# S5 tables built inside the RWKV chain of a hybrid decoder layer, and S5 inputs projected earlier

## The chip, the core and the metric

One NeuronCore of one Trainium2 chip runs the whole layer. The metric is device time in microseconds (us), the median of three runs of the same kernel: 1288.53 us before the change (1288.47 to 1292.1). A prediction is for the same metric of the changed kernel on the same kind of chip.

## What the reference computes

One decoder layer on x of shape (1, 1024, 1024) in float32. A normalised input goes through one combined projection; four head groups of 256 channels use it, their outputs are concatenated and projected, and a squared-ReLU MLP follows:

```python
h = rmsnorm(x, norm_mix_pre[l])
proj = h @ w_in
out_s5 = s5_mixer(s5_u, ...)
out_ret = retention_mixer(ret_q, ret_k, ret_v, ret_g, cos, sin)
out_rw, v_first = rwkv7_mixer(rw_cols, ...)
out_sb = stick_breaking_mixer(sb_q, sb_k, sb_v)
mixed = jnp.concatenate([out_s5, out_ret, out_rw, out_sb], axis=-1) @ w_out[l]
x = x + rmsnorm(mixed, norm_mix_post[l])
h = rmsnorm(x, norm_ffn_pre[l])
f = jnp.square(jax.nn.relu(h @ w_up[l])) @ w_down[l]
x = x + rmsnorm(f, norm_ffn_post[l])
```

The S5 mixer is a complex diagonal recurrence over the sequence, followed by a GELU and a gated linear unit. The kernel does it in blocks of 8 tokens: with powers of the complex diagonal in two tables (RC the real, RS the imaginary part, 128 positions each) the recurrence becomes a real scan between two rotations.

## The kernel before

The program is one long list of instructions that a tile scheduler distributes over the engines. Each engine, and each queue of DMA issues (nearly all are issued by SyncE, "SP"), then works through its own list strictly in order. So an instruction that waits holds back all that stands behind it on its engine.

The order of the stages is this. The input is normalised and transposed (tiles hh and hl, the high and low part of each float32 number). The RWKV columns are projected first. Then comes the RWKV chain: 16 chunks of 64 tokens, one `rwkv_chain` each (lines 587 to 630), a recurrence whose small matmuls (tiles cr, cu, cs, cy) depend on one another over ScalarE, VectorE and GpSimd. During the first half of the chain a second triangular inverse is made (`rwkv_inverse`, lines 507 to 529: VectorE's loop, a store to DRAM, a load back as tile tx, matmuls ix). Then `rwkv_out` (lines 633 to 664) finishes RWKV's two halves of tokens; after that the kernel takes turns between two Python generators, `retention` and `s5_main`, for 14 rounds (lines 2005 to 2015), and goes on with the stick-breaking attention (tiles z, om, be, wt), the output projection and the MLP.

What TensorE does between the links of these chains is filler: the rest of the input projection. It comes from `proj_rest` (six channel groups, then three token groups with index 1, 2, 0, which are retention's v, S5's input u, and the attention's v; then the attention's k and q). Each product is three float32-replicated matmuls (`mm3`, lines 131 to 133). The class `Pace` hands the filler out in small portions (`g.pace.fill(n)`) and counts them in `g.pace.n`: 131 portions when the chain ends, 147 after `rwkv_out`. In the loop of 14 rounds `s5` takes part only once `g.pace.n` has reached 164, that is from the fifth round on.

On-chip memory is handled as slots of [128, 1024] float32, s0 to s40, lent by `M.get(group, ...)` and given back by `M.put`. Twenty of them (s21 to s40) belong to group "R" during RWKV; after `rwkv_out` ten go to "rt" (retention) and ten to "s5". A slot that is lent again makes its new user wait for its last user.

In the first step of `s5_main` the kernel loads u twice (tile un, named s5n; line 1115), copies it (us, line 1117), transposes it with TensorE (s5p, line 1124; uT, line 1125), loads the two tables QT (line 1129) into slots that un has given back, and builds RC and RS on GpSimd: seven doublings, each one complex multiplication (`cmul`, lines 892 to 906), 44 instructions with the two memsets. The second step multiplies QT by uT on TensorE (s5p, line 174 in `Traced`) and VectorE multiplies the result by RC and RS (lines 1164 to 1170).

Of the kernel before, what the change touches and what calls it, by code (L numbers as in the profile page):

```python
# [181 lines left out]
def flat(ap):  # L182
    return ap.rearrange("p a b -> p (a b)")
# [917 lines left out]
def s5_main(tc, g, I):  # L1101
# [10 lines left out]
    us = [M.get(G, [128, 8, 8, 16], F32, "s5u") for _ in range(2)]  # L1112
    for b in range(2):
        un = M.get(G, [128, 8, 8, 16], F32, "s5n")
        SY.dma_start(un.rearrange("p j g c -> p j (g c)"),
                     g.d_u.rearrange("(p j) x -> p j x", j=8)[:, :, 128 * b:128 * b + 128])
        V.tensor_copy(us[b], un.rearrange("p j g c -> p g j c"))
        M.put(un)
    uT = [M.get(G, [128, 8, 128], F32, "s5uT") for _ in range(2)]
    for g0 in range(0, 16, 4):  # L1120
        ps = psw()
        for q in range(4):
            gg = g0 + q
            T.transpose(ps[:, q], us[gg // 8][:, gg % 8].rearrange("p j c -> p (j c)"), g.ident)
        A.activation(uT[g0 // 8][:, g0 % 8:g0 % 8 + 4], ps, AF.Copy)
    M.put(*us)
    QT = [M.get(G, [128, 8, 128], F32, "QT") for _ in range(2)]
    for ri in range(2):
        SY.dma_start(flat(QT[ri]), g.d_qt[ri])

# [12 lines left out]
    M.put(W1, W2)  # L1143
    RH = M.get(G, [128, 8, 128], F32, "RH")
# [660 lines left out]
def kernel(ctx: ExitStack, tc: tile.TileContext, I, out, dbg=None):  # L1805
# [71 lines left out]
    def proj_rest():  # L1877
        for j, col in ((0, 256), (1, 384), (2, 512), (3, 640), (4, 1024), (5, 1152)):
            yield from proj_ch(tc, g, I, col, sink_plain(tc, g, g.d_ret[128 * j:128 * j + 128]))
        yield from proj_tok(tc, g, I, 1, tok, sink_tok(tc, g, g.d_vr))  # L1880
        yield from proj_tok(tc, g, I, 2, tok, sink_tok(tc, g, g.d_u.rearrange("(u p) c -> p u c", p=128)))
# [86 lines left out]
    P.memset(g.ST, 0.0)  # L1968
    ys = []
# [4 lines left out]
    for c in range(NCH):  # L1974
# [11 lines left out]
        if c % 8 == 7:  # L1986
            t = c // 8
            ys.append(g.y)
            M.put(g.AR[0][t], g.AR[1][t], g.BK[0][t], g.BK[1][t], g.UV[2 * t], g.UV[2 * t + 1], g.Aq[t])
    for t in range(2):  # L1990
        rwkv_out(tc, g, t, ys[t])
        g.pace.fill(8)
# [7 lines left out]
    rt, s5 = retention(tc, g, I), s5_main(tc, g, I)  # L2000
    g.we = "AV"
    g.T = Traced(T)
# [8 lines left out]
    for i in range(14):  # L2011
        paced(rt)
        if g.pace.n >= 164:
            paced(s5)
# [184 lines left out]
```

## Time and profile before

| what | value |
|---|---|
| median of the runs | 1288.53 us (1288.47 to 1292.1) |
| the profiled execution | 1289.48 us |
| its span | 1287.3 us |
| mean granted TensorE clock in it | 0.989 |
| TensorE busy | 1233.5 us, 96% of the span |
| VectorE, ScalarE, GpSimd busy | 68%, 47%, 12% |

How to read it: a busy TensorE is one that has a matmul in its pipeline, at whatever clock. The granted clock (PEclk) is a share of the full 2.4 GHz; at 1.2 GHz it reads 0.5. A window of 10 us with 0.83 has thus spent about a third of its time at the lower level. A wait is named by who waited and who released it. Rows of a timeline give start, length, engine, line, operation, tiles and shapes, and in brackets the idle time before it with its releaser; SPq rows are DMA issues, and their length is the time that the issue kept the queue.

### The profile page before, as it was taken

To read this page: it belongs to the slowest core of one execution; us is meant where nothing else is said; L and a number is where in the kernel's file an instruction comes from. 1 tells how busy PE (TensorE), PEld (TensorE's weight loads), DVE (VectorE), ACT (ScalarE), POOL (GpSimd) and SP (SyncE) were. 2 spreads that over 40 slices of the span, in tenths; PEclk is the share of its full clock that TensorE was granted. 3 is DMA by queue.
4 is the path that set the end of the run, shared out by engine and by line. 5 is a ranking of instruction groups with operands and counts; after the bars stand their busy time and mean duration, and the time that the engine had idled before them with its cause. 6 is when DMAs were issued, how large, how long until landed. Compare 5 with 4: busy or idle time off the path is not lost.

```text
span 1287.3 us, 19608 instructions
## 1 busy us (share of the span) xinstructions
PE 1233.5 (96%) x7256; PEld 993.3 (77%) x7256; DVE 870.8 (68%) x1724; ACT 607.8 (47%) x1152; POOL 152.5 (12%) x181
## 2 busy tenths in 40 slices
PE   4999998999989999999999999999999999999997
PEld 4788776778877756778787888888888788888885
DVE  8884676623555236789889768876758576776757
ACT  6453351262412344466666645454555433554541
POOL 1332011102351102433400000000000000000000
PEclk9999998999998999999999999999999999999999
DMA  5121242224655457433541378653379653444433
GB/s 203 66 82 70 74 109 80 76 91 137 197 147 95 148 162 227 126 103 95 163 157 42 99 220 294 212 164 123 138 248 325 219 157 123 115 123 151 146 122 146
DMA packets 129375, 185.93 MB, mean 144 GB/s; under 512 B 37456, under 2 KB 63552, under 8 KB 129280
## 3 DMA queue, kind: packets, MB, share of 16 engines
q1 hardware_dynamic: 129280, 184.68, 45.4%
q8 instruction: 57, 0.93, 0.3%
q14 instruction: 38, 0.31, 0.1%
HBM read 125.94 MB, written 58.70 MB: 143 GB/s over the span
## 4 chain that ended last, share of the span: by engine, by line
PE 71%; DVE 13%; DMA 8%; ACT 4%; issue 2%; POOL 1%; SPq 0%; DVEq 0%; ACTq 0%
PE pu_b L1416 19%; PE pd_b L1701 18%; PE mm_b L131 6%; PE mm_b L132 5%; PE mm_b L133 5%; PE pd_b L1757 3%; DVE om_s L722 2%; DMA wraw_s<-in_w_in_dram 1%; PE mmc_b L131 1%; DMA wraw_s<-in_w_up_dram 1%; PE mmc_b L132 1%; PE mmc_b L133 1%; PE av_b L757 1%; DVE v_s L1385 1%; PE s5p_b L174 1%
## 5 line engine op out<-in xcount | busy, mean ns | idle before, releaser
L1416 PE MATMUL pu_b<-v_s,v_s 128*128 128x512 f32 x1344 | 306.9, 390 | 0.7 <-DVE u_h L1560 0.5
L1416 PEld LDWEIGHTS pu_b<-v_s,v_s 128*128 128x128 f32 x1344 | 251.8, 188 | 54.0 <-DVE u_h L1560 0.9
L1701 PE MATMUL pd_b<-v_s,v_s 128*128 128x512 f32 x1152 | 262.2, 389 | 2.5 <-ACT v_s L1384 2.5
L1701 PEld LDWEIGHTS pd_b<-v_s,v_s 128*128 128x128 f32 x1152 | 216.0, 188 | 48.2 <-ACT v_s L1384 3.3
L131 PE MATMUL mm_b<-hh_s,wh_s 128*128 128x512 f32 (+1 forms) x296 | 122.7, 415 | 1.2 <-DVE xs_s L359 0.5
L132 PE MATMUL mm_b<-hl_s,wh_s 128*128 128x512 f32 (+1 forms) x296 | 117.4, 397 | 0.0
L133 PE MATMUL mm_b<-hh_s,wl_s 128*128 128x512 f32 (+1 forms) x296 | 115.7, 391 | 0.0
L1384 ACT ACTIVATE v_s<-wd_s 128x512 fp32r<-128x512 f32 x112 | 68.2, 623 | 67.9 <-PE pd_b L1701 30.3
L1385 DVE TENSOR_TENSOR v_s<-wd_s,v_s 128x512 fp32r<-128x512 f32 x112 | 75.6, 685 | 22.8 <-ACT v_s L1384 22.2
L1384 ACT ACTIVATE v_s<-fl_h 128x512 fp32r<-128x512 f32 x96 | 59.4, 625 | 66.5 <-PE pd_b L1701 29.4
L1384 ACT ACTIVATE v_s<-wraw_s 128x512 fp32r<-128x512 f32 x96 | 59.0, 628 | 63.7 <-PE pu_b L1416 44.6
L1385 DVE TENSOR_TENSOR v_s<-fl_h,v_s 128x512 fp32r<-128x512 f32 x96 | 65.6, 686 | 30.3 <-ACT v_s L1384 29.7
L1385 DVE TENSOR_TENSOR v_s<-wraw_s,v_s 128x512 fp32r<-128x512 f32 x96 | 65.7, 693 | 16.3 <-ACT v_s L1384 15.9
L131 PEld LDWEIGHTS mm_b<-hh_s,wh_s 128*128 128x128 f32 x296 | 56.6, 191 | 18.0 <-issue 2.4
L133 PEld LDWEIGHTS mm_b<-hh_s,wl_s 128*128 128x128 f32 x296 | 56.7, 191 | 13.5 <-issue 2.0
L132 PEld LDWEIGHTS mm_b<-hl_s,wh_s 128*128 128x128 f32 x296 | 56.9, 192 | 12.1 <-issue 3.0
L1680 DVE TENSOR_TENSOR wd_s<-wd_s,wd_s 128x512 f32<-128x512 f32 x64 | 41.8, 686 | 29.9 <-DMA wd_s<-in_w_down_dram 29.6
L267 DVE TENSOR_TENSOR wl_s<-wraw_s,wh_s 128x1024 fp32r<-128x1024 f32 x28 | 37.3, 1331 | 36.4 <-ACT wh_s L264 36.3
L131 PE MATMUL mm_b<-wh_s,hh_s 128*128 128x256 f32 x192 | 59.3, 310 | 0.0
L133 PE MATMUL mm_b<-wh_s,hl_s 128*128 128x256 f32 x192 | 56.1, 292 | 0.0
L132 PE MATMUL mm_b<-wl_s,hh_s 128*128 128x256 f32 x192 | 56.0, 292 | 0.0
L722 DVE TENSOR_TENSOR_SCAN om_s<-om_s 128x128 f32<-128x128 f32 (+7 forms) x32 | 46.1, 1440 | 13.9 <-ACT om_s L718 13.5
(399 smaller groups left out, 2159.8 us busy)
## 6 DMA issues: line engine op xcount, KB each, us to landing
fl_h<-d_f SPq DMA_DIRECT2D x96, 256.0 KB, 3.2
wraw_s<-in_w_up_dram SPq DMA_DIRECT2D x32, 512.0 KB, 4.4
wd_s<-in_w_down_dram SPq DMA_DIRECT2D x64, 256.0 KB, 3.8
wraw_s<-in_w_in_dram SPq DMA_DIRECT2D x21, 512.0 KB, 3.9
d_f<-u_h SPq DMA_DIRECT2D x32, 256.0 KB, 3.4
d_f<-fa_h SPq DMA_DIRECT2D x28, 256.0 KB, 3.6
d_f<-p_h SPq DMA_DIRECT2D x28, 256.0 KB, 3.2
xt_s<-in_x_dram SPq DMA_DIRECT2D x8, 512.0 KB, 8.4
```

What stands on the lines that cost most here:

```text
L131: return [nc.tensor.matmul(ps, ah, bh, start=start, stop=False, **k), nc.tensor.matmul(ps, ah, bl, start=False, stop=False, **k), nc.tenso ...
L132: nc.tensor.matmul(ps, ah, bl, start=False, stop=False, **k),
L133: nc.tensor.matmul(ps, al, bh, start=False, stop=stop, **k)]
L174: self.ins = self.t.matmul(*a, **k)
L267: i = (nc.gpsimd if lo_eng == "P" else nc.vector).tensor_tensor(wl, raw, wh.bitcast(F32), ALU.subtract)
L722: V.tensor_tensor_scan(rev, rev, rev, 1.0, ALU.mult, ALU.bypass)
L1384: nc.scalar.activation(v[:, 0], src, AF.Copy)
L1385: self.low = nc.vector.tensor_tensor(v[:, 1], src, v[:, 0].bitcast(F32), SUB).ins
L1416: nc.tensor.matmul(ps, v[:, a, ks], h[:, b], start=start and k == 0 and x == 0, stop=k == 3 and x == 2, skip_group_check=True)
L1680: V.tensor_tensor(blk(o, p), blk(a, p), blk(b, p), SUB)
L1701: nc.tensor.matmul(banks[q], v[:, a, qs], w[:, b], start=fresh and p == 0 and x == 0, stop=p == 15 and x == 2, skip_group_check=True)
L1757: nc.tensor.matmul(ps, v[:, a], w[:, b], start=False, stop=p == 15 and x == 2, skip_group_check=True)
```

## The change

`s5_main` is cut differently. Its first step now only takes slots for RC, RS and two work tiles and builds the tables. This step is run inside the chain loop, right behind chunk 7, with four "R" slots that the first half of the chain has given back. Its second step then loads u and QT, into slots that are no longer shared with each other, transposes u and goes on as before. `proj_rest` projects u ahead of retention's v. The loop of 14 rounds lets `s5` take part from `g.pace.n` 136 on, which is its first round.

```diff
     RC, RS = (M.get(G, [128, 8, 128], F32, n) for n in ("RC", "RS"))
     W1, W2 = (M.get(G, [128, 1024], F32, n) for n in ("s5a", "s5b"))
...
+    for lv in range(7):
+        s = 1 << lv
+        cmul(P, RC[:, :, s:2 * s], RS[:, :, s:2 * s], RC[:, :, 0:s], RS[:, :, 0:s], b3(g.rot[:, lv, 0], s),
+             b3(g.rot[:, lv, 1], s), v3(W1, s), v3(W2, s))
+    M.put(W1, W2)
+    yield
+    un = [M.get(G, [128, 8, 8, 16], F32, "s5n") for _ in range(2)]
     us = [M.get(G, [128, 8, 8, 16], F32, "s5u") for _ in range(2)]
     for b in range(2):
-        un = M.get(G, [128, 8, 8, 16], F32, "s5n")
-        SY.dma_start(un.rearrange("p j g c -> p j (g c)"),
+        SY.dma_start(un[b].rearrange("p j g c -> p j (g c)"),
                      g.d_u.rearrange("(p j) x -> p j x", j=8)[:, :, 128 * b:128 * b + 128])
-        V.tensor_copy(us[b], un.rearrange("p j g c -> p g j c"))
-        M.put(un)
+        V.tensor_copy(us[b], un[b].rearrange("p j g c -> p g j c"))
+    M.put(*un)
+    QT = [M.get(G, [128, 8, 128], F32, "QT") for _ in range(2)]
+    for ri in range(2):
+        SY.dma_start(flat(QT[ri]), g.d_qt[ri])
     uT = [M.get(G, [128, 8, 128], F32, "s5uT") for _ in range(2)]
...
     M.put(*us)
-    QT = [M.get(G, [128, 8, 128], F32, "QT") for _ in range(2)]
-    for ri in range(2):
-        SY.dma_start(flat(QT[ri]), g.d_qt[ri])
...
     def proj_rest():
...
+        yield from proj_tok(tc, g, I, 2, tok, sink_tok(tc, g, g.d_u.rearrange("(u p) c -> p u c", p=128)))
         yield from proj_tok(tc, g, I, 1, tok, sink_tok(tc, g, g.d_vr))
-        yield from proj_tok(tc, g, I, 2, tok, sink_tok(tc, g, g.d_u.rearrange("(u p) c -> p u c", p=128)))
...
+    g.T = Traced(T)
...
+            if t == 0:
+                M.move("R", "s5", 4)
+                s5 = s5_main(tc, g, I)
+                next(s5)
...
-    rt, s5 = retention(tc, g, I), s5_main(tc, g, I)
+    rt = retention(tc, g, I)
     g.we = "AV"
-    g.T = Traced(T)
...
     for i in range(14):
         paced(rt)
-        if g.pace.n >= 164:
+        if g.pace.n >= 136:
             paced(s5)
```

The count of instructions stays the same to within one on each engine; what changes is their order, and which slot each tile has. Three places matter below. In these rows a tile's name ends with its slot or bank and a running number (tx_s31 lies in slot s31, cs_b5 in PSUM bank b5), and what an instruction waits for on other engines or DMA queues stands in brackets.

The first place is TensorE's list in chunk 6 of the chain, where the ix matmuls of the second inverse read tx. Before:

```order
L616 MATMUL cs_b5_2625<-UV_s26_1558,BKt_h12_2543 64x64 [waits Activation_49]
L568 MATMUL cy_b7_2633<-Gr_h5_2529,UV_s26_1558 64x64
L616 MATMUL cs_b5_2625<-UV_s26_1558,BKt_h12_2543 64x64 [waits DVE_49]
L616 MATMUL cs_b5_2625<-UV_s26_1558,BKt_h12_2543 64x64 x2
L568 MATMUL cy_b7_2633<-Gr_h11_2530,UV_s26_1558 64x64
```

and in the changed kernel:

```order
L616 MATMUL cs_b5_2625<-UV_s26_1558,BKt_h12_2543 64x64 [waits Activation_49]
L568 MATMUL cy_b7_2633<-Gr_h5_2529,UV_s26_1558 64x64
L522 MATMUL ix_b2_2176<-tx_s31_2169,Aq_s24_2057 32x32 [waits DMAHW2_49]
L616 MATMUL cs_b5_2625<-UV_s26_1558,BKt_h12_2543 64x64 [waits DVE_49]
L616 MATMUL cs_b5_2625<-UV_s26_1558,BKt_h12_2543 64x64 x2
L568 MATMUL cy_b7_2633<-Gr_h11_2530,UV_s26_1558 64x64
```

The first of the ix matmuls, which waits for the load of tx, has moved up 19 places; the other 31 follow 16 places below it.

The second place is where S5's first product stands. On SP's queue of the changed kernel the two loads of QT come in these rows:

```order
L661 DMA d_mx_63<-o_bo_s21_3461 128x512 [waits DMAHW0_49,DVE_49]
L346 DMA d_vr_61<-stg_h2_3634 128x512 [waits Activation_49]
L787 DMA rx_s21_3868<-d_ret_57 128x1024 [waits DMAHW2_49,DMAHW0_49]
L260 DMA wraw_s18_3745<-in_w_in2_dram 128x1024 [waits PE_49]
L1263 DMA xr_x0_4879<-in_x_dram 128x1024 [waits DMAHW4_49,DVE_49]
L1136 DMA QT_s36_3595<-d_qt_72 128x1024 [waits DMAHW5_49,DVE_49]
L1136 DMA QT_s22_3596<-d_qt_72 128x1024 [waits DMAHW6_49,PE_49]
```

and on TensorE's list of the changed kernel (slot s36 was until then lent to o_q of `rwkv_out`'s last step, which L655 reads last):

```order
L133 MATMUL mm_b1_3637<-wh_s16_3338,hl_s13_132 128x256
L659 MATMUL ow_b3_3491<-o_sg_s22_3459,pk_s30_398 128x512 [waits DVE_49]
L174 MATMUL s5p_b6_3694<-s5uT_s29_3599,QT_s36_3595 64x128 [waits DMAHW5_49,PE_49,Activation_49]
L174 MATMUL s5p_b6_3694<-s5uT_s29_3599,QT_s36_3595 64x128 x3
L174 MATMUL s5p_b6_3694<-s5uT_s29_3599,QT_s36_3595 64x128 [waits Activation_49]
```

Before the change 33 rows lay between that L659 and the first product of QT; now they are neighbours, and the second load of QT takes the slot s22 that this very L659 reads.

The third place is the end of the interleaved rounds. ScalarE's list in the changed kernel, where retention's last normalisation (rsg, rms) stands among the attention's z:

```order
L264 ACTIVATE wh_s17_4663<-wraw_s24_4661 128x1024 [waits DMAHW3_49,Activation_49]
L878 ACT_TABLE_LOAD
L878 ACTIVATE rsg_h5_4522<-rms_b7_4617,der_113 128x512 [waits PE_49]
L878 ACTIVATE rsg_h13_4527<-rms_b4_4618,der_113 128x512 [waits PE_49]
L718 ACT_TABLE_LOAD [waits DVE_49]
L718 ACTIVATE om_s30_4714<-z_b3_4715 128x128 [waits PE_49]
L719 ACTIVATE be_s32_4713<-z_b3_4715 128x128 [waits DMAHW7_49]
L879 ACT_TABLE_LOAD
L879 ACTIVATE rsg_h5_4522<-rsg_h5_4522 128x512 [waits Activation_49]
L879 ACTIVATE rsg_h13_4527<-rsg_h13_4527 128x512 [waits Activation_49]
L740 ACTIVATE wt_s37_4706<-wtp_b6_4707 128x128 [waits DMAHW7_49,PE_49]
L718 ACT_TABLE_LOAD
```

and TensorE's beside it:

```order
L174 MATMUL rms_b4_4618<-rsg_h13_4527,pk2_400 128x512 [waits Activation_49]
L713 MATMUL z_b3_4715<-sbk_s31_4634,sbq_s25_4635 128x128 [waits Activation_49]
L715 MATMUL z_b3_4715<-sbk_s31_4634,sbq_s25_4635 128x128
L717 MATMUL z_b3_4715<-rr_404 128x128
L713 MATMUL z_b2_4741<-sbk_s36_4631,sbq_s26_4697 128x256 [waits DMAHW5_49,DMAHW4_49,Activation_49]
L715 MATMUL z_b2_4741<-sbk_s36_4631,sbq_s26_4697 128x256
L717 MATMUL z_b2_4741<-rr_404 128x128
L713 MATMUL z_b3_4771<-sbk_s22_4632,sbq_s26_4697 128x256 [waits Activation_49]
```

Before, S5's gated unit (gl, L1233) stood between these rms and the z; it now stands well ahead of them, and the z follow the rms directly. The last row here reuses bank b3, so it waits for L719 of z_b3_4715 on ScalarE.

## Rows read from the trace of the kernel before

**Rows 1.** The page, part 1: busy time and share of the span of each engine.

```profile
PE 1233.5 (96%) x7256; PEld 993.3 (77%) x7256; DVE 870.8 (68%) x1724; ACT 607.8 (47%) x1152; POOL 152.5 (12%) x181
```

**Rows 2.** Windows: length, busy PE, PEld, DVE, ACT, POOL; PEclk, DMA share, GB/s.

```profile
345.00:425.00 80.00, 70.16 (x549) 60.42 (x548) 42.85 (x69) 23.06 (x30) 26.60 (x46) 0.91 0.54 140
425.00:500.00 75.00, 69.96 (x378) 49.52 (x376) 26.73 (x40) 29.55 (x49) 5.05 (x5) 1.00 0.52 165
...
360.00:370.00 10.00, 6.66 (x61) 6.33 (x62) 2.77 (x8) 3.11 (x5) 9.42 (x14) 0.83 0.58 170
380.00:390.00 10.00, 8.18 (x82) 7.32 (x81) 10.00 (x20) 2.51 (x3) 1.97 (x1) 0.78 0.70 121
390.00:400.00 10.00, 10.00 (x79) 9.10 (x78) 9.78 (x10) 2.21 (x3) 3.17 (x3) 0.88 0.74 129
410.00:420.00 10.00, 7.40 (x60) 6.13 (x59) 1.99 (x3) 3.98 (x6) 0.00 (x0) 0.83 0.16 54
```

**Rows 3.** Waits of TensorE from 320 to 520 us: us in total, times, longest.

```profile
PE s5p_b L174 <- DMA QT_s<-d_qt: 3.2, 1, 3.2
PE gl_b L174 <- ACT s5sg_h L1233: 2.4, 1, 2.4
PE rs_b L174 <- DVE s5e_h L1169: 1.8, 1, 1.8
...
PE mmc_b L131 <- POOL mxh_h L1269: 1.5, 1, 1.5
...
PE s5p_b L178 <- DVE s5u_s L1117: 1.0, 1, 1.0
```

**Rows 4.** Timeline of TensorE, SP's queue and VectorE around chunk 6.

```profile
246.95 1.45 SPq L645 DMA_DIRECT2D o_bo_s<-d_bo  x1
246.97 1.08 DVE L508 COPY ai_s<-tw_s 32x1024 f32<-32x1024 f32 x1
248.50 0.38 SPq L509 DMA_DIRECT2D d_t<-ai_s  x1
251.75 0.96 SPq L515 DMA_DIRECT2D tx_s<-d_t  x2
251.37 0.34 PE L616 MATMUL cs_b<-UV_s,BKt_h 128*64 128x64 f32 x4
254.49 0.24 PE L522 MATMUL ix_b<-tx_s,Aq_s 32*32 32x32 f32 x2
```

**Rows 5.** DMA issues: count, KB each, median us from issue to landing.

```profile
QT_s<-d_qt SPq DMA_DIRECT2D x2, 512.0 KB, 4.4
...
tx_s<-d_t SPq DMA_DIRECT2D x4, 64.0 KB, 2.6
...
d_t<-ai_s SPq DMA_DIRECT2D x2, 128.0 KB, 2.7
```

**Rows 6.** Timeline of GpSimd: its step in the chain, and the tables' last instruction.

```profile
272.05 0.40 POOL L602 TENSOR_TENSOR SP<-ST,PL 128x128 f32<-128x128 f32 x1 [8.40 <-DVE ST L620]
...
371.41 1.29 POOL L906 TENSOR_TENSOR RS_s<-s5a_s,s5b_s 128x512 f32<-128x512 f32 x1
```

**Rows 7.** Timeline of VectorE and TensorE from the end of `rwkv_out`.

```profile
354.53 0.69 DVE L655 TENSOR_TENSOR y_s<-ow_b,o_q_s 128x512 f32<-128x512 f32 x1 [1.50 <-ACT o_q_s L654]
355.28 1.13 PE L659 MATMUL ow_b<-o_sg_s,pk_s 128*128 128x512 f32 x2 [0.41 <-DVE y_s L655]
365.26 1.98 PE L174 MATMUL s5p_b<-s5uT_s,QT_s 128*64 128x128 f32 x16 [3.19 <-DMA QT_s<-d_qt]
```

**Rows 8.** Timeline of ScalarE at retention's last step; L264 by the groups of lines.

```profile
L264 ACT ACTIVATE wh_s<-wraw_s 128x1024 fp32r<-128x1024 f32 x12 | 12.7, 1057 | 23.6 <-DMA wraw_s<-in_w_out_dram 12.4 <-DMA wraw_s<-in_w_in_dram 9.7 <-PE mm_b L133 1.5
...
473.90 1.28 ACT L878 ACT_TABLE_LOAD   x1 [7.01 <-PE rms_b L174]
475.19 1.26 ACT L878 ACTIVATE rsg_h<-rms_b,der 128x512 f32<-128x512 f32 x2
476.47 1.28 ACT L718 ACT_TABLE_LOAD   x1
477.77 0.28 ACT L718 ACTIVATE om_s<-z_b 128x128 f32<-128x128 f32 x1
```

More of the change, by code (lines that the diff above doesn't have):

```diff
@@ L1111, in s5_main @@
     W1, W2 = (M.get(G, [128, 1024], F32, n) for n in ("s5a", "s5b"))
-    us = [M.get(G, [128, 8, 8, 16], F32, "s5u") for _ in range(2)]
-    for b in range(2):
-        un = M.get(G, [128, 8, 8, 16], F32, "s5n")
-        SY.dma_start(un.rearrange("p j g c -> p j (g c)"),
-                     g.d_u.rearrange("(p j) x -> p j x", j=8)[:, :, 128 * b:128 * b + 128])
-        V.tensor_copy(us[b], un.rearrange("p j g c -> p g j c"))
-        M.put(un)
[L1119 to L1126, printed above, removed]
-    QT = [M.get(G, [128, 8, 128], F32, "QT") for _ in range(2)]
-    for ri in range(2):
-        SY.dma_start(flat(QT[ri]), g.d_qt[ri])
     def b3(x, k):
@@ L1143, in s5_main @@
     M.put(W1, W2)
+    yield
+    un = [M.get(G, [128, 8, 8, 16], F32, "s5n") for _ in range(2)]
+    us = [M.get(G, [128, 8, 8, 16], F32, "s5u") for _ in range(2)]
+    for b in range(2):
+        SY.dma_start(un[b].rearrange("p j g c -> p j (g c)"),
+                     g.d_u.rearrange("(p j) x -> p j x", j=8)[:, :, 128 * b:128 * b + 128])
+        V.tensor_copy(us[b], un[b].rearrange("p j g c -> p g j c"))
[3 more added lines that the diff above has]
+        SY.dma_start(flat(QT[ri]), g.d_qt[ri])
+    uT = [M.get(G, [128, 8, 128], F32, "s5uT") for _ in range(2)]
+    for g0 in range(0, 16, 4):
+        ps = psw()
+        for q in range(4):
+            gg = g0 + q
+            T.transpose(ps[:, q], us[gg // 8][:, gg % 8].rearrange("p j c -> p (j c)"), g.ident)
+        A.activation(uT[g0 // 8][:, g0 % 8:g0 % 8 + 4], ps, AF.Copy)
+    M.put(*us)
     RH = M.get(G, [128, 8, 128], F32, "RH")
```

## The prediction

> **What bounds the kernel now.** I read the page's busy times first: TensorE is busy for 1233.5 of 1287.3 us [rows 1], so it sets the time, and no other engine comes near. Matmuls are neither added nor taken away. So the change can only act on two things: TensorE's idle time, and the time at which it runs at half its clock. Second come the windows over the stretch that the change reorders [rows 2]: from 345 to 425 us TensorE is idle for 80 − 70.16 = 9.84 us, from 425 to 500 us for 75 − 69.96 = 5.04. The granted clock is 0.91 in the first of these and 1.00 in the second. Four windows of 10 us inside it read 0.83, 0.78, 0.88 and 0.83; at 0.5 for the slow part, a share s of slow time gives 1 − s/2, and what is lost against full speed is half of s, that is 10 × (1 − clock) = 1.7 + 2.2 + 1.2 + 1.7 = 6.8 us at most. Third, the list of waits says who is late [rows 3]: S5's chain in the first stretch (QT's load 3.2, rs behind VectorE's S5 work 1.8, the copies of u 1.0) and in the second the gated unit behind ScalarE (gl, 2.4) and the first output projection (mmc, 1.5). So at most 15 us of idle time and 7 us of clock are within reach, 1.7% of the run.
>
> **The tables: 0 us.** GpSimd now builds RC and RS during chunks 8 to 11. The work is all that stands on it between 350 and 372.7 us, some 22 us; the last instruction of it takes 1.29 us [rows 6]. In the chain GpSimd idles 8.40 us between its steps [rows 6], and the step has that whole time until VectorE needs it. The order puts 13 of the 44 instructions at most between two steps, about 10 us by the long ones; the step behind them comes up to 2 us later than now and is still some 6 us early. Were this cover gone, each us of lateness would appear at the next cs and cr. Taken at 0, between 0 and 2.
>
> **The chain: +1.8 us.** The first ix matmul now stands before three of the four cs matmuls of chunk 6 (first place of the change). It needs tx. Before, TensorE reached that cs at 251.37 and the ix only at 254.49, without a wait [rows 4]. In the new order the store of d_t no longer has a 1.45 us load (o_bo) ahead of it on SP, so it leaves when VectorE's copy ends, at 246.97 + 1.08 = 248.05 instead of 248.50. It lands 2.7 later, 250.75, and the load of tx 2.6 after that [rows 5], 253.35. TensorE arrives at about 251.5, so it waits 1.8. Behind the ix stand the rest of cs, VectorE's new state and so the whole chain; nothing else can run on TensorE in that time. Bounds: 1.2 (a faster store) to 2.9 (tx as late as the 254.49 at which it was surely there).
>
> **The stretch from 345 to 425 us: 9.84 → 7.5, −2.3 us.** The waits of rs on S5's VectorE work and on the gelu go, because S5 now starts ahead of retention and has no GpSimd work behind it. QT's wait does not go. QT now has slots of its own among S5's tiles, but slot s36 was lent until then to o_q of `rwkv_out`, whose last reader is L655 at 354.53 + 0.69 = 355.2 [rows 7]. SP then issues the load, 0.3, and it lands 4.4 later [rows 5], at 359.9. On TensorE the product of QT comes directly behind the L659 that waits for the same L655 (second place). That L659 starts at 355.28 now [rows 7]; one of its two matmuls later, at 355.9, TensorE has nothing until 359.9: 4.0 us in place of the 3.2 [rows 3]. Between 3.3, if SP is free at once and the load is quicker, and 5. Four small waits are new or remain: L659 on VectorE, the second `rwkv_out` square behind a memset that waits for GpSimd, the transposes of u on VectorE's copies (1.0 before [rows 3]), retention's rkv behind the later v. The trace has no such waits alone; each is bounded by 0 and by the 1.8 of rs [rows 3], and I take 0.9: 3.5 together. 4.0 + 3.5 = 7.5.
>
> **The stretch from 425 to 500 us: 5.04 → 9.5, +4.4 us.** S5's gated unit finishes early, so its 2.4 [rows 3] goes. But the last normalisation of retention now sits among the attention's z (third place). There each logarithm and exponential needs another function table than the attention, and TensorE has no filler between them. The row of rms waits for a square behind a weight conversion of 1.06 us (L264 [rows 8]); with its load I take 1.4. Then the third z waits for its bank b3 until ScalarE has done: the table load 1.28, two logarithms 1.26, a table load 1.28, and two evictions of 0.28 [rows 8], 4.4 us; another L264 of 1.06 ahead makes 5.4. TensorE's own z work covers 0.3: 5.1. A later z waits behind a second pair of loads with the exponentials; most of that is covered by attention filler, 1.6. The output projection's 1.5 stays at about 1.4. The sum is 1.4 + 5.1 + 1.6 + 1.4 = 9.5, between 5 (retention's squares come a few us before TensorE gets there, as ScalarE was idle for 7.01 us ahead of this step [rows 8]) and 11.
>
> Here the trace speaks of what a switch costs. The load ends at 477.75 and the eviction behind it starts at 477.77 [rows 8], so a switch is 1.28 us and nothing more. The Trainium skill, page "ScalarE: Activation LUTs", section "What ACT_TABLE_LOAD costs", puts a switch at some 2.66 us, 1283 ns for the load and some 1380 ns of drain. By it four switches in this place would cost 5.5 us more, an estimate, and the time would be near 1298. The load's length agrees with the trace; the drain beside it is not visible there, so the sum goes by 1.28.
>
> **The clock: 0.** In the trace the clock falls to 0.83 in the window with the wait of 3.2 us and stays at 1.00 with the 2.4 [rows 2, 3]. The new waits of 4.0 and 5.1 replace those of 3.2 and the rs pair as occasions. I leave the 6.8 us as they are, with −6.6 and +4 as bounds. The rest of the diff (u before v in the projection, the earlier `Traced`) moves filler of equal length and costs nothing by itself; v's load being late is among the small waits.
>
> **Sum.** 1.8 − 2.3 + 4.4 + 0 = +3.9 us against the profiled execution's 1289.48, so 1293.4. That execution was 0.95 above the median of 1288.53, so against the median the change gives **1292.4**.
>
> **Rivals.** A measurement of this kernel can tell about 0.3%, 3.9 us, from no change; so faster is under 1284.7 and slower over 1292.4.
> - *A, faster, 0.27:* S5's earlier start frees ScalarE at the end. The point that decides is whether ScalarE has finished retention's squares before TensorE reaches rms; then the z never queue behind the tables, and the tail keeps only 1.5 + 1.1. With the rs waits gone the two windows at 0.78 and 0.88 also read near 1, −3.4. Then +1.8 − 2.3 − 2.4 − 3.4 = −6.3, 1282. For it speaks that ScalarE is busy only 29.55 of 75 us there [rows 2]; against it that each table load stands in order ahead of evictions that z needs.
> - *B, no change, 0.21:* the change does not do what it says, because QT is held by o_q and S5 gets no further ahead than now; waits only change names, ±2, 1288.5. For it: the wait for QT is the same size in my sum; against it: u's loads leave some 30 us earlier.
> - *C, much slower, 0.18:* each new wait (ix, QT, z) is followed by a stretch at half clock as after the 3.2 one. Three times 1.7 us [rows 2] on top of the sum, 1297.5. The page's rule on switches would come out at the same place.
> - *The forecast, 0.34:* 1288.5 to 1296 by the bounds of its terms, half of it above 1292.4.
>
> **Numbers.** Faster is A, 0.27. The same is B and the lower half of the forecast, 0.21 + 0.17 = 0.38. Slower is the upper half and C, 0.17 + 0.18 = 0.35. The range of 8 in 10 goes from A's 1282 to 1298 and leaves out the faster part of A and the slower part of C. The forecast's own range is 1288.5 to 1296.
>
> **What the profile of the changed kernel would show.** GpSimd's tables between 263 and 300 us and no wait of TensorE on them or on its step. A wait of ix on tx of about 1.8 in chunk 6. A wait of s5p on QT of about 4.0 near 356 us, and none of rs on S5. A wait of z on L719 of about 5 near 480 us, with table loads of L878, L718, L879, L718 in a row before it. I am wrong if the z wait is missing (then A), if the sum of idle time from 345 to 500 us is below 12 us, or if the clock in the four windows departs from 6.8 us lost by more than 3.

## The result and the profile after

The changed kernel is slower: 1298.11 us (1296.87 to 1300.42, 4 runs) against 1290.32 for the kernel before beside it on the same chip; over the undisturbed executions of both the ratio is 1.0071 [1.0048, 1.0095]. The profiled execution took 1300.42 us with a span of 1298.6, 11.3 longer than before; it is the slowest of the four, 2.3 above their median, so the sums below, which come from one execution of each kernel, hold some of that spread. The page's first part [rows 1] shows the same instructions, and TensorE busy for 5.4 us longer:

```profile
PE 1238.9 (95%) x7256; PEld 995.7 (77%) x7256; DVE 868.4 (67%) x1724; ACT 608.6 (47%) x1152; POOL 151.2 (12%) x181
```

To find where the time went, both spans are cut at instructions that do the same work in both: the first cu matmul of chunks 6, 8 and 15, and one product of the attention's weights and values (av, L757 before) 1344 matmuls later. Windows of the kernel before (columns as in rows 2):

```profile
250.10:268.60 18.50, 18.50 (x348) 14.84 (x348) 4.05 (x9) 9.94 (x22) 2.88 (x6) 1.00 0.40 107
268.60:317.90 49.30, 49.30 (x575) 40.20 (x574) 14.53 (x34) 19.14 (x39) 8.20 (x11) 1.00 0.36 113
317.90:540.80 222.90, 206.65 (x1344) 163.95 (x1343) 114.28 (x174) 86.59 (x145) 55.70 (x77) 0.97 0.55 159
...
365.16:368.57 3.41, 3.31 (x29) 3.22 (x30) 1.63 (x3) 0.00 (x0) 3.25 (x4) 0.50 0.25 38
385.64:392.47 6.83, 6.83 (x38) 6.49 (x36) 6.83 (x12) 2.51 (x3) 2.10 (x1) 0.50 0.88 114
416.36:419.77 3.41, 3.41 (x21) 2.69 (x18) 1.29 (x2) 1.38 (x3) 0.00 (x0) 0.50 0.00 0
```

(the last three are all of the third stage that stood at half clock) and of the changed kernel, with two 10-us windows inside its third stage and, as the last four, all of that stage at half clock:

```profile
251.60:272.30 20.70, 19.54 (x349) 15.33 (x348) 4.05 (x9) 9.73 (x22) 7.32 (x27) 1.00 0.26 60
272.30:321.60 49.30, 49.30 (x575) 40.19 (x574) 14.68 (x34) 19.16 (x39) 16.74 (x28) 1.00 0.41 129
321.60:553.30 231.70, 209.63 (x1344) 165.07 (x1343) 111.93 (x174) 87.35 (x146) 41.80 (x37) 0.95 0.51 152
...
490.00:500.00 10.00, 4.13 (x14) 3.02 (x15) 5.45 (x11) 9.06 (x17) 0.41 (x1) 0.63 0.32 81
500.00:510.00 10.00, 10.00 (x44) 7.55 (x43) 6.13 (x10) 4.62 (x12) 1.64 (x2) 0.86 0.43 135
...
359.48:366.31 6.83, 4.60 (x37) 4.18 (x38) 3.66 (x7) 1.09 (x2) 0.00 (x0) 0.50 0.50 181
386.79:390.20 3.41, 3.41 (x18) 3.41 (x18) 1.51 (x3) 0.00 (x0) 0.00 (x0) 0.50 0.83 81
492.60:502.84 10.24, 5.40 (x16) 4.25 (x16) 4.53 (x8) 8.11 (x13) 0.41 (x1) 0.50 0.31 104
519.91:523.32 3.41, 3.41 (x9) 2.28 (x11) 3.41 (x4) 2.01 (x3) 3.24 (x3) 0.50 0.57 195
```

From chunk 6 to 8 the changed kernel takes 20.70 us in place of 18.50 (+2.2). From chunk 8 to 15, where GpSimd now builds the tables (16.74 us busy in place of 8.20), it takes 49.30 in both. The third stage takes +8.8: TensorE idles 231.70 − 209.63 = 22.07 us in place of 16.25 (+5.8), and the same 1344 matmuls keep it busy 3.0 longer. The clock is 0.95 in place of 0.97, but half clock costs only where TensorE is busy: 3.31 + 6.83 + 3.41 = 13.6 us before, 4.60 + 3.41 + 5.40 + 3.41 = 16.8 after. Half of the difference, 1.6 us, is the lower clock; where the other 1.4 of the 3.0 come from, the trace does not show. That makes 11.0; what is left, +1.5 ahead of chunk 6 and −1.2 behind the third stage, is spread: the runs below, with the same work up to there, reach chunk 6 between 248.9 and 253.4 us.

TensorE's waits name who was late. In the changed kernel, from 240 to 360 and from 360 to 530 us (columns as in rows 3):

```profile
PE ow_b L652 <- DVE s5x_s L1151: 1.8, 1, 1.8
PE ow_b L648 <- ACT o_q_s L653: 1.3, 1, 1.3
PE ow_b L659 <- DVE y_s L655: 1.2, 1, 1.2
PE ix_b L522 <- DMA tx_s<-d_t: 1.2, 1, 1.2
...
PE s5p_b L174 <- ACT s5uT_s L1143: 4.3, 1, 4.3
PE z_b L713 <- ACT be_s L719: 4.1, 2, 3.0
PE s5p_b L174 <- DMA d_vs<-stg_h: 2.2, 1, 2.2
PE wtp_b L739 <- DVE rsg_h L881: 1.9, 1, 1.9
PE z_b L715 <- DMA sbq_s<-d_sq: 1.6, 1, 1.6
PE rms_b L174 <- ACT rsg_h L873: 1.4, 1, 1.4
PE z_b L713 <- DMA sbq_s<-d_sq: 0.8, 1, 0.8
```

In the middle the wait of 4.3 us stands where S5's first product stands, as forecast; but the trace names ScalarE's copy of uT and not the load of QT. The timelines of SP, VectorE and ScalarE around it (columns as in rows 4):

```profile
356.26 1.51 SPq L1136 DMA_DIRECT2D QT_s<-d_qt  x2
355.54 0.69 DVE L655 TENSOR_TENSOR y_s<-ow_b,o_q_s 128x512 f32<-128x512 f32 x1 [0.25 <-ACT o_q_s L654]
360.35 0.68 DVE L660 TENSOR_TENSOR o_bo_s<-ow_b,y_s 128x512 f32<-128x512 f32 x1
361.06 1.09 ACT L1143 ACTIVATE s5uT_s<-s5p_b 128x512 f32<-128x512 f32 x2 [3.98 <-DVE o_bo_s L660]
```

Both are late. QT is issued when L655 has read o_q (355.54 + 0.69 = 356.23) and the first load lands 5.1 us later, at 361.4. The slot of uT was lent to y of `rwkv_out`, whose last reader L660 ends at 361.03. The product starts at 361.71.

In the tail, ScalarE's timeline shows the forecast's third place as it was foreseen, one table load after another (before: [rows 8]):

```profile
490.70 1.06 ACT L264 ACTIVATE wh_s<-wraw_s 128x1024 fp32r<-128x1024 f32 x1
491.78 1.28 ACT L878 ACT_TABLE_LOAD   x1
493.07 1.27 ACT L878 ACTIVATE rsg_h<-rms_b,der 128x512 f32<-128x512 f32 x2
494.36 1.28 ACT L718 ACT_TABLE_LOAD   x1
495.65 0.28 ACT L718 ACTIVATE om_s<-z_b 128x128 f32<-128x128 f32 x1
495.82 0.27 ACT L719 ACTIVATE be_s<-z_b 128x128 f32<-128x128 f32 x1
496.11 1.28 ACT L879 ACT_TABLE_LOAD   x1
497.41 1.15 ACT L879 ACTIVATE rsg_h<-rsg_h 128x512 f32<-128x512 f32 x2
499.69 1.28 ACT L718 ACT_TABLE_LOAD   x1
```

Each load starts where the last activation ends (490.70 + 1.06 = 491.76, then 491.78) and ends where the next one starts (491.78 + 1.28 = 493.06, then 493.07). The Trainium skill, page "ScalarE: Activation LUTs", section "What ACT_TABLE_LOAD costs", puts 1380 ns of drain beside each load; this trace leaves no room for it, ahead of the load or behind it. TensorE meanwhile goes through five waits within 14 us (sbq 1.55, rms 1.43, sbq 0.83, z 2.98, wtp 1.85; together 8.6), and the clock falls: 0.63 and 0.86 in the two windows from 490 us on, where the kernel before stayed at 1.00 up to 500 us [rows 2].

### The profile page after: what moved, and what is told of

Read it like the earlier page. It is cut to its first block, busy times and chain, and to the rows that moved or that the text cites. A ratio compares the mean times of both kernels' runs of the same rounds, so it can differ in the third digit from the quotient of the medians.

```text
span 1298.6 us, 19590 instructions
## 1 busy us (share of the span) xinstructions
PE 1238.9 (95%) x7256; PEld 995.7 (77%) x7256; DVE 868.4 (67%) x1724; ACT 608.6 (47%) x1152; POOL 151.2 (12%) x181
## 4 chain that ended last, share of the span: by engine, by line
PE 70%; DVE 14%; DMA 8%; ACT 3%; issue 3%; SPq 1%; POOL 0%; DVEq 0%; ACTq 0%
PE pd_b L1702 20%; PE pu_b L1417 16%; PE mm_b L131 5%; PE mm_b L132 4%; PE mm_b L133 4%; PE pd_b L1758 3%; DMA wraw_s<-in_w_up_dram 2%; PE mmc_b L131 2%; PE mmc_b L133 2%; PE mmc_b L132 2%; DVE om_s L722 1%; PE av_b L757 1%; PE gl_b L174 1%; DMA wraw_s<-in_w_in_dram 1%; PE ro_b L174 1%
## 5 line engine op out<-in xcount | busy, mean ns | idle before, releaser
L1386 DVE TENSOR_TENSOR v_s<-wd_s,v_s 128x512 fp32r<-128x512 f32 x112 | 75.6, 686 | 22.8 <-ACT v_s L1385 22.2
L131 PEld LDWEIGHTS mm_b<-hh_s,wh_s 128*128 128x128 f32 x296 | 57.4, 194 | 18.1 <-issue 2.4
L133 PEld LDWEIGHTS mm_b<-hh_s,wl_s 128*128 128x128 f32 x296 | 57.3, 194 | 13.3 <-issue 1.8
L131 PE MATMUL mmc_b<-wh_s,mxh_h 128*128 128x512 f32 x128 | 53.1, 420 | 0.7 <-POOL mxh_h L1270 0.6
```

Of the source, the lines that this page charges most:

```text
L131: return [nc.tensor.matmul(ps, ah, bh, start=start, stop=False, **k), nc.tensor.matmul(ps, ah, bl, start=False, stop=False, **k), nc.tenso ...
L133: nc.tensor.matmul(ps, al, bh, start=False, stop=stop, **k)]
L1386: self.low = nc.vector.tensor_tensor(v[:, 1], src, v[:, 0].bitcast(F32), SUB).ins
```

## The experiments

Three things could be behind it. *The gate*: with `s5` in every round S5 ends early, retention ends last and alone, and its normalisation lies bare among the attention's z. *The slots*: at the start S5 inherits slots that `rwkv_out` still holds. *The ix*: the chain's 2.2 us. All runs at a glance; "6 to 8" is chunk 6 to chunk 8, "idle" and "busy" are TensorE's from chunk 15 to pu, the first product of the MLP's up-projection (a longer stage than the third one above), both from the profiled execution; the ratio is to the kernel before on the same chip, with its 95% interval. The kernel before had medians of 1287.93 to 1288.57 us beside these runs, so that medians may be compared across them; the runs of one kernel spread by some 2 us about their mean, and a difference of medians of less than about 2.5 us is not told from that. The profiled execution need not be typical: that of e9 lies 5.0 below its median, that of e2 3.4 below.

| run | gate | other edit | median us | ratio | 6 to 8 | idle | busy |
|---|---|---|---|---|---|---|---|
| before | 164 | | 1288.57 | 1 | 18.5 | 17.3 | 323.3 |
| after | 136 | | 1298.11 | 1.0071 [1.0048, 1.0095] | 20.7 | 22.8 | 326.2 |
| e1_live_turns | 136 | s5 for 10 rounds | 1293.37 | 1.0045 [1.0023, 1.0067] | 20.5 | 19.4 | 325.7 |
| e2_gate164 | 164 | | 1284.05 | 0.9961 [0.9941, 0.9981] | 20.4 | 14.5 | 316.7 |
| e3_tables_only | 164 | only the tables moved | 1285.40 | 0.9980 [0.9963, 0.9997] | 20.6 | 13.3 | 322.3 |
| e5_s5_first | 136 | free slots to S5 | 1295.23 | 1.0056 [1.0039, 1.0073] | 20.8 | 17.6 | 324.5 |
| e7_both | 136 | e1 and e5 | 1290.86 | 1.0017 [0.9996, 1.0038] | 20.3 | 14.6 | 325.0 |
| e8_gate158 | 158 | | 1296.97 | 1.0062 [1.0041, 1.0083] | 20.6 | 22.9 | 323.0 |
| e6_gate164_s5first | 164 | free slots to S5 | 1296.38 | 1.0073 [1.0046, 1.0100] | 20.5 | 25.8 | 322.6 |
| e9_no_switch | 136 | Sigmoid for Ln, Exp | 1294.14 | 1.0044 [1.0025, 1.0062] | 20.5 | 18.1 | 323.9 |
| e16_both_no_switch | 136 | e7 and e9 | 1291.24 | 1.0021 [1.0009, 1.0034] | 20.4 | 14.8 | 325.1 |
| e10_ix_late | 164 | ix behind cr of chunk 7 | 1281.88 | 0.9954 [0.9938, 0.9970] | 17.9 | 15.8 | 318.6 |
| e11_exp_first | 164 | Exp before sigmoids | 1281.29 | 0.9943 [0.9924, 0.9962] | 20.7 | 13.4 | 319.0 |
| e12_both | 164 | e10 and e11 | 1279.91 | 0.9935 [0.9915, 0.9955] | 17.9 | 14.9 | 317.7 |
| e13_gate172 | 172 | | 1277.16 | 0.9910 [0.9888, 0.9931] | 23.0 | 9.0 | 318.4 |
| e14_gate172_ix | 172 | ix behind cr of chunk 7 | 1273.06 | 0.9874 [0.9855, 0.9893] | 17.9 | 8.8 | 318.3 |
| e15_before_gate172 | 172 | kernel before | 1273.53 | 0.9881 [0.9864, 0.9898] | 18.5 | 10.6 | 317.2 |

**The change with only its gate put back.**

```diff
-        if g.pace.n >= 136:
+        if g.pace.n >= 164:
```

> The changed kernel with the old gate of 164: S5 joins in the fifth round again; tables in the chain, u before v and the new slots stay. T: the filler lasts as before (24 turns of 4), the end is as before, no half clock after 490 us: 1287 to 1292, what is left being the 1.2 us of ix. R: also back, 1288 to 1291. S: QT is in its slot long before the fifth round, the wait of 4.3 us goes: 1288 to 1293. If it stays above 1295, none of the three holds and the cause lies in the chain.

1284.05 us: faster than before, and 14 us faster than the change. It lies about 3 us below the lowest of the three ranges: none had counted on a gain. Putting the gate back takes away the whole loss, and with the gate at 164 everything else in the diff together is a small gain.

**The tables alone, on the kernel before.** The diff is the kernel before with the first step of `s5_main` cut off behind the tables and run at chunk 7; u, QT, `proj_rest` and the gate stay as they were.

> The kernel before with one part of the change: the tables are built in the chain; u after v, the slots of un and QT shared, gate 164 as before. All theories: GpSimd's 44 instructions cost nothing in the chain except for the ix that moves up, +1.2 us; the wait of rs on S5 (1.8) may go. 1287 to 1292, within 0.3% of before. If it is slower by over 4 us, the tables in the chain are the cause.

1285.40, slightly faster and 1.6 below the range. The tables cost nothing in the chain, and without GpSimd's work the stage from chunk 15 to pu idles 13.3 us in place of 17.3. The 2.1 us between chunks 6 and 8 are there as well, so the ix comes with this part of the change.

**S5 only as long as it has steps.** By the kernel's own count there are 241 − 147 = 94 portions of filler behind `rwkv_out`, four to a turn. S5 has ten steps. With the gate at 136 it is given 14 turns, and the last four hand out filler while it has nothing to do: 28 turns of 4 are 112, more than 94, so the filler is gone two rounds before the end.

```diff
-        if g.pace.n >= 136:
+        if i < 10:
```

> The changed kernel, but S5 takes a turn only in the ten rounds in which it has a step left, so that a finished S5 hands out no filler. Theory T (the filler of the interleaved rounds runs out too soon, the last retention step stands bare, TensorE waits about 9 us between 480 and 500 us and then runs at half clock): the waits of z, wtp and rms in that stretch fall from 8.7 us to 5 or less and the half-clock stretches after 490 us (490:500 at 0.63, 500:510 at 0.86, 520:530 at 0.83, together 6.8 us) go; 1298.1 - 4 to - 10, so 1288 to 1294. Rival R (the earlier start of S5 itself costs, by VectorE and DMA work ahead of retention): the end stalls all the same, 1296 to 1300. Rival S (the late slots of QT and uT cost it): unchanged too, within 2 us of 1298.1.

1293.37: in the range, 4.7 us of the gate's 14, but not for the whole reason. The tail still waits 8.0 us, under other names. TensorE's waits from 440 to 540 us:

```profile
PE wtp_b L739 <- DVE rsg_h L881: 3.5, 1, 3.5
PE z_b L713 <- DMA sbq_s<-d_sq: 3.0, 2, 1.8
PE av_b L757 <- ACT wt_s L740: 1.5, 1, 1.5
```

So filler that lasts longer helps, and retention still ends alone: S5's last product gl ends at 465.4 us, and retention's last rms at 483.0.

**Slots that are free given to S5 first.**

```diff
-    M.move("R", "rt", 10)
-    M.move("R", "s5")
+    M.move("R", "s5", 6)
+    M.move("R", "rt")
```

> The changed kernel with the order of two moves of slots swapped: S5 gets the six slots that RWKV gives back first, retention the ten later ones. QT then lies in s24 and s32, uT in s40 and s35, and both are there before L655 of the last half. S: the wait of 4.3 us at the first product of QT goes, and with it the half clock of 357 to 364 us (3.4 us): 1290.5 to 1294. T: only these go, the end stays as it is with its 8.7 us and the half clock: 1291 to 1296. Rival: the wait moves to retention, whose loads now have the late slots: within 2 us of 1298.1.

1295.23, 2.9 less than the change; with the two intervals of the table overlapping, this gain alone is not clear of the spread. The wait of s5p is gone and the stage idles 5.2 us less, but a new wait takes most of its place, because retention now gets the slots that are late. From 345 to 430 us:

```profile
PE rw_b L178 <- DVE rx_s L794: 3.4, 1, 3.4
```

**Both.** The two edits above together.

> The changed kernel with both repairs, the gate at 136 as in the change: S5 takes turns only while it has steps (1293.4 alone), and S5 gets the early slots (1295.2 alone). If the two costs add (4.7 and 2.9): 1290 to 1291.5. T and S: no wait at QT, half the waits at the end; still 5 us or more above the kernel with gate 164 (1284.05). Rival, that an early start is as good as a late one once its two accidents are gone: 1282 to 1286.

1290.86. The gains add up as far as the spread lets it be told (4.7 and 2.9 alone, 7.2 together), as they do for two causes and not for one. The kernel is still 7 us slower than with the gate at 164: of the gate's 14 us about half lies in neither. In the table the two idle for the same time (14.6 and 14.5), so in these executions the difference is busy time, 325.0 against 316.7. Most of it is clock: TensorE was busy at half clock for 3.41 + 5.46 + 6.73 = 15.6 us here and for 3.4 at 164, which is 6.1 us of the 8.3. The idle time is the same in sum, but here it comes in fewer and longer waits (3.7, 3.5 and 3.0, against 2.6 and 1.8 at 164).

**The function tables taken out of the tail.** Retention's Ln and Exp, in both halves of the tokens, become Sigmoid, which the attention uses too; what this leaves out is the value of retention's normalisation.

```diff
-        in_turn(tc, [A.activation(sgs[m], pss[m], AF.Ln, bias=g.eps6, scale=1.0 / 64) for m in range(2)] +
-                [A.activation(sgs[m], sgs[m], AF.Exp, scale=-0.5) for m in range(2)])
+        in_turn(tc, [A.activation(sgs[m], pss[m], AF.Sigmoid, bias=g.eps6, scale=1.0 / 64) for m in range(2)] +
+                [A.activation(sgs[m], sgs[m], AF.Sigmoid, scale=-0.5) for m in range(2)])
```

> The changed kernel with retention's logarithm and exponential (L878, L879) replaced by the sigmoid that the attention uses, so that ScalarE needs no other function table there; what is left out is the true value of retention's normalisation, all instructions but the table loads stay, in the same order on TensorE. Theory T (the z of the attention wait behind ScalarE's table loads and two logarithms): the waits of z on L719 (3.0) and of wtp (1.9) fall to 1 in sum or less, the stretch at half clock after 490 us (10.2 us) gets shorter or goes; 1298.1 - 4 to - 9: 1289 to 1294. Were a switch 2.66 us, as the page of the Trainium skill on ScalarE's tables has it, the same waits would have been longer than measured by 1.38 for each switch. Rival R (the earlier start costs for lack of cover, whatever function ScalarE runs): the waits move to other instructions of the same stretch, 1296 to 1299.

1294.14, just outside the range of T, and 4.0 faster than the change. The wait of z on L719 shrinks from 4.1 in two to 1.5 in two, wtp's from 1.9 to 0.8, and the window behind them reads 0.83 where the change had 0.63:

```profile
490.00:500.00 10.00, 10.00 (x42) 7.52 (x41) 6.92 (x12) 3.75 (x11) 1.55 (x2) 0.83 0.51 163
```

So by the medians these table loads cost about 4 us with the half clock that they bring, not 14. The same edit on top of the two others:

> The kernel of e7_both (early gate, both repairs, 1290.9) with retention's logarithm and exponential replaced by the attention's sigmoid; left out is the true value of retention's normalisation. Theory T (retention ends last, and its table loads among the z are what is left of the loss): the wait of wtp (3.5) falls to about 1 and one of the two half-clock stretches of 6.8 us at the end goes: 1284 to 1288. Theory R (missing cover, whatever the functions): 1289 to 1292.

1291.24, no gain that can be told (1290.86 without it). The rest is not ScalarE's tables. The waits from 460 to 530 us, and behind them the window that holds them, show a tail that waits instead for the attention's loads and for retention's last product:

```profile
PE z_b L713 <- DMA sbq_s<-d_sq: 6.3, 2, 3.3
PE wtp_b L739 <- DVE rsg_h L881: 2.1, 1, 2.1
```

```profile
480.00:490.00 10.00, 4.85 (x16) 2.93 (x14) 2.89 (x6) 3.13 (x7) 0.00 (x0) 0.79 0.57 194
```

**The dose of the gate.** First half-way, at 158, then past the old value, at 172 (the diff is the number alone).

> The changed kernel with the gate at 158, so that S5 joins in the third round, between 136 (first round, 1298.1) and 164 (fifth, 1284.05). R (what S5 does early is missing as cover at the end, so the loss grows with each round of lead): about half way, 1289 to 1294. S alone (only the first round meets the late slots of QT): near 1284 to 1288. T alone (26 turns of 4 use up the filler one round too soon): 1288 to 1293.

1296.97, a miss: nearly as slow as 136. Its waits from 345 to 540 us begin with the same z:

```profile
PE z_b L713 <- ACT be_s L719: 6.7, 3, 3.4
PE s5p_b L174 <- DMA TZ_s<-d_k: 5.1, 1, 5.1
```

Here too S5 waits at its start, for another load (TZ, 5.1). From 136 to 158 nothing is gained that can be told, and from 158 to 164 it is 13 us, so the loss does not shrink round by round. Counting the rounds from 0, at 158 S5's steps end in round 11 and retention's in round 13; at 164 both end in round 13; at 172 S5 has only rounds 6 to 13, and its last two steps come behind the loop and behind retention's last logarithm and exponential.

> Gate 172: S5 joins in the seventh round, two later than with 164, so that retention's last normalisation is over before the attention's z begin and S5's last steps stand at the end. Theory R (each step of S5 is cover for a wait of retention and the other way round; what matters is that both end together): S5's last steps now stand bare, waits of gl and s5p of 3 us or more with half clock behind them, 1287 to 1292. Rival (only retention's table loads among the z hurt): the end gets shorter, 1279 to 1284.

1277.16: 7 us faster than 164 and 21 faster than the change. Theory R fell; the rival had the direction right, and the gain was larger than its range. The waits from 345 to 515 us have none over 0.9 us in the tail (first fence), and ScalarE's timeline (second) shows what changed: retention's two table loads come well ahead of z, and from S5's gated unit (L1234) on, which has the attention's table, no load stands between the evictions of z. S5's gl (460.4 to 476.4 us) is also at work then, as cover between the z; no run parts these two:

```profile
PE ow_b L652 <- DVE o_bo_s L660: 1.9, 1, 1.9
PE z_b L713 <- DMA sbq_s<-d_sq: 1.2, 2, 0.9
```

```profile
449.94 1.28 ACT L878 ACT_TABLE_LOAD   x1
...
453.46 1.28 ACT L879 ACT_TABLE_LOAD   x1
...
461.28 1.28 ACT L1234 ACT_TABLE_LOAD   x1
...
468.10 0.28 ACT L718 ACTIVATE om_s<-z_b 128x128 f32<-128x128 f32 x1 [0.88 <-PE z_b L717]
```

The order on TensorE goes with the time. In the change and in e1, e5, e7, e8, e9 and e16 S5's gl is over 6 to 10 us before the first z, and retention's last rms ends 7 to 10 us behind it (change: gl to 472.7, z from 481.6, rms to 491.3). In the kernel before and in all runs at 164 gl lasts for 12 to 15 us beyond the first z, and rms ends with it (e2: 482.1, 467.5, 468.1); of these only e6 is slow, by a wait at its start. At 172 rms is over at 451.2, the first z comes at 466.9, and gl lasts to 476.4.

**The slots at the gate of 164.** The slot edit of above, with S5 in its old place.

> The gate of 164 with the swapped slots, S5's early, retention's late. At gate 164 nothing waits for QT, but TensorE waits for L659 (1.3), L652 (1.8) and the copies of u (1.4), and retention's loads now come later. S5's copies are early: -1.4; L659 as with the swap at gate 136, -1.3; retention's rx late: up to +3.4. 1281 to 1286. If it is above 1286, the swap only moves a wait.

1296.38, a miss of 10 us. S5 holds slots that it does not need for four rounds, and retention, which starts first, gets those that `rwkv_out` holds to its end, so its loads come late. The longest wait from 345 to 480 us, and then the windows around it:

```profile
PE rw_b L178 <- DVE rx_s L794: 15.0, 2, 13.8
```

```profile
360.00:370.00 10.00, 0.00 (x0) 0.00 (x0) 2.45 (x2) 0.00 (x0) 3.67 (x2) 0.61 0.96 311
370.00:380.00 10.00, 5.26 (x27) 4.86 (x28) 9.22 (x9) 0.29 (x1) 2.45 (x2) 0.54 0.32 104
```

Free slots belong to whoever starts first; who that is depends on the gate.

**The ix put back.** At the gate of 164 the ix matmuls are ordered behind chunk 7's first matmuls (cr) by an ordering without a semaphore (`g.ix` lists them).

```diff
+        if c == 7:
+            gate, g.pace.gate = g.pace.gate, g.pace.marks[-3]
+            g.pace.behind(g.ix)
+            g.pace.gate = gate
```

> Gate 164 (1284.05) with one more order: the ix matmuls of the second inverse come behind the cr of chunk 7, about where they stood before the change. Theory C (the ix that moved up costs the chain its wait of 0.8 to 1.2 us and another us of disorder, 1.8 to 2.3 us from chunk 6 to chunk 8 in each variant so far): chunk 8 starts as early as before, 1281.5 to 1283. Rival: only the wait itself counts, 1283 to 1284; if above 1285, the matmuls behind cr hold back cu in turn.

1281.88, 2.2 less than at 164 alone, which by itself is within the spread. No wait of ix is left, and chunk 6 to 8 takes 17.9 us in place of 20.4: the trace shows the chain's part of the loss.

**Retention's Exp ahead of the sigmoids.** At the gate of 164 the attention's first sigmoids are held behind retention's last Exp (`g.turn` is retention's list of four activations), which saves one table load.

```diff
-            A.activation(om[:, b0:b0 + n], z[:, 0:n], AF.Sigmoid, scale=-0.125)
+            y = A.activation(om[:, b0:b0 + n], z[:, 0:n], AF.Sigmoid, scale=-0.125)
+            if s < 4:
+                in_turn(tc, [g.turn[-1], y])
```

> Gate 164 with one more order on ScalarE: the attention's first sigmoids come behind retention's last exponential, not between its logarithm and its exponential. One table load fewer (1.28 us) stands ahead of S5's gate: the wait of gl (2.56 us) falls to about 1, and the half clock of 3.4 us at 477 us goes: 1280.5 to 1283. Rival: TensorE has nothing else then and waits at z for the same time: 1283.5 to 1286.

1281.29, 2.8 less than at 164 alone, hardly more than the spread; gl's wait falls from 2.6 to 1.5 in two. With the ix put back as well:

> Both orders on top of gate 164. If they add: 1278.5 to 1282, and the clock stays at 1.00 from 345 us to the end of the attention. Rival: the gains overlap or a new wait takes their place: 1282 to 1284.

1279.91: 4.1 less than at 164 alone, where the two gains would add to 5.0; that difference is within the spread.

**The best version, and what of it is the change's.** The change with the gate at 172 and the ix put back:

> The change with gate 172 and the ix matmuls behind the cr of chunk 7. The two add: 1277.2 - 2.2 to - 5 (in the one profile of e13 chunks 6 to 8 took 23.0 us, against 20.4 to 20.8 in the others and 17.9 with ix behind cr): 1272 to 1275. If the gains overlap: 1276 to 1278.

1273.06, 1.3% faster than before. And the kernel before with nothing but its gate set to 172:

> The kernel before with one number changed, the gate 172 in place of 164; tables built by S5's first step after the chain, as before. If the gate alone gives the gain of e13 (retention's normalisation is over before the z begin): as much as from gate 164 to 172 with the change, 1288.2 - 7, so 1279 to 1284. If the tables' 22 us of GpSimd then come too late and S5 ends bare: 1286 to 1291.

1273.53, 5.5 us below the lower of the two ranges. The gate alone does it. With the gate at 172 the change as it was written is 3.7 us behind this (0.9910 against 0.9881 of 1288, with overlapping intervals), its chain from chunk 6 to 8 at 23.0 us in place of 18.5; in that execution the window from 250 to 260 us reads 0.83, where e1 and e10 have 1.00, so part of the 23.0 is clock. With the ix put back it is level: 0.5 us apart, inside the spread of either (1271.42 to 1273.74 and 1272.25 to 1274.88).

## Why the prediction was wrong

The forecast was 1292.4; measured were 1298.11, which is 0.1 us above the range and near rival C's 1297.5. The likeliest case had the sign of its sum right, and three of its five terms; two steps failed.

- **"The tables: 0 us" held.** From chunk 8 to 15 it is 49.30 us before and after, and the tables alone made the kernel slightly faster. GpSimd's last table instruction ends at 289.6 us, within the stretch named.
- **"The chain: +1.8 us" held:** +2.2, of which 1.16 is the named wait of ix on tx, and the rest lies in the cs and cr behind it. With the ix put back, this stretch is 2.5 shorter at 164 (e10).
- **"9.84 → 7.5, −2.3 us" failed.** The named waits of this stretch (`rwkv_out` to retention's ro, those over 0.3 us) sum to 9.8 us before and 10.8 after: +1.0. The wait for S5's first product was foreseen (4.0, measured 4.3), but the step counted only QT's slot. uT's slot was held just as long by L660, and VectorE had retention's rx (L793, L794) in its list ahead of L660. And the "four small waits of 0.9" came out as 1.2 (L659), 1.8 (L652, behind the memset), 1.3 (L648, behind ScalarE) and 2.2 (S5's product with TZ, L174); the last two are not among those named. Together they are 6.5 and not 3.5, nearer to four times the bound of 1.8 than to half of it.
- **"5.04 → 9.5, +4.4 us" held in size:** the waits of 0.3 us and more from the first z to the output projection's mmc sum to 5.9 before and 10.9 after, +5.0. Inside the term the parts differ. rms was 1.4 as taken. ScalarE's part took 4.3 from the end of L264 (491.76) to that of the eviction (496.09), as summed, but the third z waited 3.0 and not 5.1: L264 ran mostly beside rms, and in the meantime TensorE had two z to do and a wait of 0.8 for a load. The 1.6 for a later z behind the exponentials came as wtp's 1.9. The sbq loads' 2.4 were not named. The place and its mechanism were right, but not that ScalarE's tables are all of it: without them 4 us of the gate's 14 came back (e9).
- **"The clock: 0" failed.** The stage's busy time rose by 3.0 us for the same matmuls, of which the lower clock explains 1.6. The bound of +4 stood in the text; the value was set to zero because a single wait of 2.4 us had left the clock at 1.00, and new waits were to take the place of old ones. In the middle they did: 8.0 us of work at half clock in place of 13.6. But 8.8 came in the tail, where there had been none: 5.4 with the five waits close together, 3.4 some 20 us later. (Reckoned as the prediction does, by 1 − clock over the whole time, the loss goes from 6.8 to 11.9; 7.1 us of the time at half clock were idle and cost nothing more.)

That the number is near rival C's is partly luck. C had a stretch at half clock behind each of the waits of ix, QT and z, at 5.1 in all. The wait of ix left the clock at 1.00, the middle lost 2.8 us less than before (half of 13.6 − 8.0), and only the tail was hit, by 4.4, so that 1.6 is left in place of 5.1; the distance to 1298 is made up by the stretch from 345 to 425 us.

Sum of the terms as measured: 2.2 + 1.0 + 5.0 + 3.0 = 11.2, against 11.3 between the two spans. The largest error is the stretch from 345 to 425 us (3.3), then the busy time (3.0). Rival A named what decides, a ScalarE that is done with retention before z needs it, but the change moved away from it: a later gate brings that about, not an earlier one (e13, e15). Rival B fell, since S5 did get further ahead: gl ends at 472.7 and not at 486.2.

What I did not weigh is that an earlier S5 is not only earlier at its start. It ends earlier too, keeps handing out filler when it has none of its own work (e1, 4.7 us), and leaves retention to end alone. That is in the loop of 14 rounds, in the code and not in any row. That the 7 us which are left in e7 come from this end is argued from the order of gl, rms and z above and from the sweep of the gate; no run changes the end alone.

The attention's loads sbq are late in e7 because q is the last of the filler: its last stores are issued at 477.90 and 479.12, the loads at 482.08, behind a wait for the stores to land, and TensorE has no step of S5 left to cover that. At 164 the stores go at 468.36 and 468.84, the loads from 473.23, and two groups of gl (at 470.57 and 476.73) stand there.

Open: whether the same holds for e16; what a gate above 172 gives; and what the gate of 136 does with u projected behind v, which was not tried, since S5 would there read u before it is stored.

## What to carry to other kernels

When two interleaved chains share one filler, look first at where each ends: let the one whose last steps share the next stage's function table and can cover its loads end last (here S5, at a gate of 172), and stop a finished one from handing out filler. Count for each slot the last reader of its previous owner, and give the free ones to whoever starts first. Price a cluster of new waits with the half clock behind it, counting only the time in which the engine is busy, and sweep the number that sets the start before building machinery around it: here one number, 164 to 172, gave 15 us, and the rewritten stage nothing that can be told on top of it.

## What the runs showed of the hardware

- Waits cost more than themselves when the clock falls behind them. Behind the start of a wait of 13.8 us the windows read 0.61 and 0.54; 17.1 us stood at half clock, TensorE was busy for 4.5 of them, so that the lower clock added 2.2 (e6). In the tail of the change it is 10.2 us at half clock, 5.4 of them busy, 2.7 added. The Trainium skill, page "TensorE: Matmul & The Clock Gate", section "HAM oscillation — how this bites in real kernels", describes a loop that pays for the lower clock after every wait; these two stretches agree with it, but not every wait here was followed by one: the 2.4 of gl left the clock at 1.00 [rows 2, 3].
- Logarithm and exponential each have a table load of 1.28 us here even when nothing of another table stands between them (449.94 and 453.46 in e13). The Trainium skill, page "ScalarE: Activation LUTs", section "Table sets: the hidden batching unit", names a set that holds both; this kernel's program did not use it.
